# RWKV-7's chunk outputs: 128-row and 64-row products issued as two runs instead of alternating

## The chip, the cores and the metric

The kernel runs on one NeuronCore of one Trainium2 chip. The metric is the device time of one execution in microseconds (us); lower is better. A time is the median of several executions. The profile is of one further execution.

## The reference, cut to what matters

The reference is a two-layer encoder on 256 tokens of 1024 features. Each layer is a SwiGLU feed-forward, then three token mixers side by side (RWKV-7, Hyena, Mamba-2 SSD) that share one input projection and one output projection, then a second SwiGLU. The change touches the RWKV-7 mixer alone, whose recurrence is, per head of 64 channels and in both directions of time:

```python
def rwkv7_step(S, inp):
    r_t, w_t, k_t, v_t, a_t, b_t = inp
    sa = jnp.einsum('dbhij,dbhj->dbhi', S, a_t)
    S = S * w_t[..., None, :] + sa[..., None] * b_t[..., None, :] + v_t[..., None] * k_t[..., None, :]
    return S, jnp.einsum('dbhij,dbhj->dbhi', S, r_t)
```

The scan runs over 256 tokens, for 8 heads and 2 directions, in each of the 2 layers. The output of a token is the state `S` applied to the receptance `r_t`.

## The kernel before, in words

Everything is kept feature-major: features on the 128 partitions, tokens along the free axis. The large projections and the feed-forwards are dense products, 128 x 128 weights against 256 tokens, each done in three passes over split operands (`mm3`, tiles named `psd` in the profile). Their weights are loaded by SyncE's queue (`raw`), rounded to the first part on ScalarE (`whi`, L278) and the second part is made on VectorE or GpSimd (`wlo`, L308).

RWKV-7 is done in chunks of 64 tokens, four chunks per sequence, and in two waves (w = 0, 1) of two head pairs each. `rw_invert` inverts the triangular blocks of a wave on GpSimd (L886, L888). `rw_chain` then goes over the four chunks, i = 0 to 3. It holds eight instances at a time: u = 0 to 3 (direction and pair) times e = 0, 1 (the head of the pair, on partitions 0 to 63 or 64 to 127; `HALF[e]`). One step i is, on TensorE,

- `pr`: eight products of 128 rows (scores against removal values and values), copied by VectorE to `rw_rhs` (L968);
- `pu`: eight products of 64 rows with the inverses `zt`, copied into `se` and `so` by VectorE (L973) and ScalarE (L974);
- `pn` (not in the last step): eight products of 128 rows, from which VectorE makes the next state `new`; VectorE and ScalarE copy it into the operands of the next step (L991, L992);
- `py`: the outputs of the chunk. For each of the eight instances one product of 128 rows (`ss` against the scores `gg`, written G below) and, from the second chunk on (`st` is not None), one product of 64 rows (the state `st` against the receptances `ar`, written S below) into the same 64 x 64 sum. ScalarE copies `py` to `yd` (L1002).

All of them are float32 and have 64 output columns; head e = 0 writes partitions 0 to 63 of the bank and e = 1 the other half. A float32 product shows as two MATMUL records and two LDWEIGHTS records in the profile, so one step's `py` is 16 products and 32 records where there is a state and 8 products and 16 records where there is none. In records the operands read as `128*64 128x64` for `pr`, `pn` and G, and as `64*64 64x64` for `pu` and S; `pu` carries the name `rw_rhs`.

The order on each engine is planned at build time: the framework takes the program order as priority, simulates the engines (`schedule_with_timeline_sim=True`, L1456) and lets independent work run between the steps of the chain. TensorE's time between them is filled with dense products of the projections and with SSD's products (`pss`). The chains run at about 423 to 487 us (layer 0, wave 0), 512 to 590 us (layer 0, wave 1), 1261 to 1327 us and 1350 to 1426 us (layer 1).

Of the kernel before, what the change touches and what calls it, by code (L numbers as in the profile page):

```python
"""Two hybrid encoder layers (SwiGLU, RWKV-7 / Hyena / SSD mixers, SwiGLU) on one core.

Everything is kept feature-major: [feature in a tile of 128, tile, token].  Products run as three
float32r passes over exactly split operands (hi * hi + hi * lo + lo * hi)."""
# [20 lines left out]
# columns of SBUF: the mixers' arena, its part that is given up after RWKV-7, a block within it, the  # L25
# arena of the set up
ARENA, AHEAD, BLK, START = 63 * 256, 65 * 256, 7 * 1024, 16 * 1024
# what outlives the part that is given up; the grid of places within an arena
KEEP, GRID = ("blk", "y0", "y1", "mg"), 256
# products of the next sublayer that start before the LayerNorm's statistics are known  # L30
NE = 4
# units of the mixers' output projection that are loaded and split ahead
NPRE = 1
# LayerNorm, by tile: h on ScalarE, the mean taken off on GpSimd; the tile whose split comes before
# the early products are made up
HACT, SUBP, EA = (0, 1, 1, 1, 0, 1, 1, 1), (0, 0, 1, 1, 1, 1, 1, 1), 3
# adaLN chunks computed alongside each sublayer; buffers for those in the mixers; rows multiplied on GpSimd
# there; tiles of ones in the start up that have buffers of their own; the output tile of a SwiGLU at which
# all have to be done
NSIDE, NRING, SPOOL, NRAW, SIDEM = (4, 2, 4, 4, 1, 1), 3, (0, 0, 0, 0, 1, 0, 1, 0), 4, 3  # L40
# order of the projections: gates, dt, SSD tiles; gates, Hyena
SEQ = ("g" * 10 + "d" + "s" * 12, "g" * 14 + "h" * 8)
# one in so many splits of weights goes to GpSimd (0: none), by part of the mixers
# [12 lines left out]
def layout(inp):  # L56
    """Inputs as DRAM arrays, moved into the order in which the kernel reads them."""
# [47 lines left out]
def constants():  # L105
    """Tables that follow from the shapes alone."""
# [36 lines left out]
class Arena:  # L143
    """A region of SBUF in which arrays are placed; the framework orders what overlaps."""

    def __init__(self, *aps):
        self.aps, self.clock = [], len(aps)
        self.holes, self.live = [], {}
        for ap in aps:
            o = self.aps[-1][0] + self.aps[-1][1] + 1 if self.aps else 0  # L150
            self.aps.append((o, ap.shape[1], ap))
            self.holes.append((o, ap.shape[1]))
        # when each column was given back last
        self.freed = np.zeros(o + ap.shape[1], int)
        for i, (o, n, _) in enumerate(self.aps):
            self.freed[o:o + n] = i

    def drop(self):
        """The last part is given up; it has to be empty."""
        o, n, _ = self.aps.pop()  # L160
        assert (o, n) in self.holes, (o, self.live)
        self.holes.remove((o, n))

    def take(self, name, shape):
# [4 lines left out]
        # the columns that have been free for longest  # L169
# [35 lines left out]
def spread(items, counts):  # L205
    """The items in order, as lists of so many each."""
    items = iter(items)
    return [[next(items) for _ in range(n)] for n in counts]


class Builder:
# [42 lines left out]
    def dbank(self):  # L254
        """A bank for one dense product."""
        return self.bank("d", 4)[:, 0:256]

# [33 lines left out]
    def mm(self, out, lhsT, rhs, start, stop):  # L291
        return self.nc.tensor.matmul(out, lhsT, rhs, start=start, stop=stop)  # L292
# [4 lines left out]
    def after(self, later, *earlier):  # L297
        """Issue order on one engine."""
        for e in earlier:
            self.tc.add_manual_dep(later.ins, e.ins.name, ORDER, reason="issue order")  # L300
# [9 lines left out]
    def unit(self, dram, width=1024, ahead=None):  # L310
        """One unit of weights, loaded and split."""
# [30 lines left out]
    def dense_pair(self, outs, ws, x):  # L342
        """Two products that follow x tile by tile as it comes."""
        for k in range(NT):
            for out, w in zip(outs, ws):
                self.mm3(out, w, k * 128, x[k], k == 0, k == NT - 1)

# [39 lines left out]
    def cond_row(self):  # L387
        """silu(c) on every partition."""
# [65 lines left out]
    # ---- residual + LayerNorm; tiles of the sublayer's output come through ln_put().  All are  # L454
    # centred by the mean of the first one's features: the mean of all differs from it by at most
    # sqrt(7) standard deviations, so that the sums of squares keep their accuracy ----
# [18 lines left out]
    def u_put(self, m):  # L475
        """The tile as it enters the products that start before the statistics are known."""
        if self.nxt in self.mods:
            assert (*self.nxt, 0) in self.done and (*self.nxt, 1) in self.done
            a, hi = self.mods[self.nxt][:, 24 + m:25 + m], self.uh[:, m, 0:256]
            self.act(hi, self.r[:, m, :], AF.Identity, scale=a)  # L480
            self.stt(self.ul[:, m, 0:256], self.r[:, m, :], a, hi.bitcast(F32), MUL, SUB)

    def early(self, units, ahead):
        """The next sublayer's first products, of a * r instead of a * (r - mean) * rstd + b; two
        more columns take -a and b through the weights, from which early_end() makes them up."""
# [9 lines left out]
    def early_end(self, mu, rs, prev):  # L495
        """(product - mu * first column) * rstd; the second column is left as a bias."""
# [9 lines left out]
    def ln_put(self, m, psum):  # L506
# [5 lines left out]
        if m == 0:  # L512
# [4 lines left out]
            # the tiles that are still to come are centred through xa  # L517
# [151 lines left out]
    def shift(self, l, dst, i, spread=False):  # L669
        """The token shift; spread: on ScalarE and GpSimd."""  # L670
# [14 lines left out]
    def conv(self, l, dst, i, wn, bn, taps, n, j):  # L685
        """A centred depthwise convolution of projection tile i; n tiles of channels, this one is j."""
# [45 lines left out]
    def rw_keys(self, s):  # L732
        """Decays, gates and keys of both directions, scaled within chunks of 64."""
# [6 lines left out]
        # normalised keys  # L740
# [25 lines left out]
        # cumulative decays in chunks of 64, taken from their middle  # L766
# [14 lines left out]
        # scaled receptances and removal keys; keys and removal values  # L781
# [8 lines left out]
        # what the bonus sums  # L790
# [7 lines left out]
    def rw_scores(self, s):  # L798
# [13 lines left out]
        for d in (0, 1):  # L812
# [17 lines left out]
            # scores  # L830
# [18 lines left out]
            # keys token-major  # L849
# [11 lines left out]
            # removal keys over the first block of the scores  # L861
# [9 lines left out]
    def rw_invert(self, s):  # L871
        """Unit triangular inverses of 32 x 32 blocks, one a lane (direction, half, instance, head)."""
# [18 lines left out]
        # zout[0]: the inverses, zout[1]: transposed  # L891
# [7 lines left out]
    def rw_chain(self, s):  # L899
# [4 lines left out]
        # values token-major  # L904
# [13 lines left out]
        # the inverses, transposed, on the diagonals of 64 x 64 blocks, and those that join them  # L918
# [16 lines left out]
        # joined into 64 x 64 blocks  # L935
# [21 lines left out]
        # the chain over four chunks  # L957
# [4 lines left out]
        for i in range(4):  # L962
# [12 lines left out]
            if i < 3:  # L975
# [5 lines left out]
                # the factor between chunk c and the next one in this direction  # L981
# [10 lines left out]
                nc.scalar.copy(out=so[64:128, :, i + 1, :], in_=new[64:128])  # L992
            py = bank("m", 2).rearrange("p (u q) -> p u q", q=64)
            for u in range(4):
                c = 3 - i if u > 1 else i
                for e in (0, 1):
                    self.mm(py[HALF[e], u, :], ss[e][:, u, i, :], gg[e][u // 2][:, u % 2, i, 64:128], True, st is None)
                    if st is not None:
                        self.mm(py[HALF[e], u, :], st[HALF[e], u, :], ar[HALF[e], u // 2, u % 2, c], False, True)
# [8 lines left out]
    def rw_out(self, s):  # L1008
        """Group norm over heads, bonus, gate."""
# [41 lines left out]
    def ssd_proj(self, l):  # L1051
# [9 lines left out]
        # dt = softplus, and the running sums of its decays within chunks of 128  # L1061
# [29 lines left out]
    def ssd_tiles(self, l):  # L1091
        """Twice the SiLU, as (1 + tanh(x / 2)) x."""
# [16 lines left out]
    def ssd(self, l):  # L1109
        nc, A, F, bank, scol = self.nc, self.A, self.F, self.bank, self.scol  # L1110
        # x * dt token-major, for each direction
        self.yc = []
        for g in (0, 1):
# [12 lines left out]
            # C B^T, masked where it is on the diagonal  # L1126
# [9 lines left out]
            for e in range(4):  # L1136
# [6 lines left out]
                for d in (0, 1):  # L1143
# [3 lines left out]
                    # from the other chunk: d = 0 from 0 into 1, d = 1 from 1 into 0  # L1147
# [32 lines left out]
    def hy_sin(self, x):  # L1180
        """sin of x in place, brought into [-pi, pi] first."""
# [20 lines left out]
    def hy_filter(self):  # L1202
        """Spectra of the filters of both layers, kept in DRAM, and their norms."""
# [101 lines left out]
    def gates(self, l):  # L1305
        """tanh(x / 2) of the gates' projections, kept in DRAM: twice the gate is one more."""
# [154 lines left out]
```

## Time and profile before

| | |
|---|---|
| time, three runs | 1717.62, 1721.4, 1725.15 us; median 1721.4 us |
| span of the profiled execution | 1726.7 us, 35017 instructions |
| TensorE (PE) busy | 1599.4 us, 93% of the span, 13142 matmul records |
| PE's weight loads (PEld) busy | 1494.3 us, 87% |
| VectorE (DVE) busy | 1319.2 us, 76% |
| ScalarE (ACT) busy | 946.2 us, 55% |
| GpSimd (POOL) busy | 599.8 us, 35% |
| chain that ended last, by engine | PE 68%, DVE 17%, DMA 5%, ACT 4%, POOL 3% |
| mean granted TensorE clock | 0.956 of full speed |

The page gives the profiled execution's span, from its first to its last instruction, and no separate time around it; the span lies 5.3 us above the median of the three runs. A busy TensorE is not a TensorE at its peak: the end of each matmul is modelled, so the pace of a run of matmuls is read from the starts, or from the chain of waits, which cuts time where the next instruction starts. The granted clock has two levels in these rows, 1.2 GHz (0.50) and 2.4 GHz (1.00); a value between them is a mix within the stretch.

### The profile page before, as it was taken

The numbers are of one execution on the slowest core, as the hardware profiler recorded it, in microseconds if no ns is written. First come the engines' busy times: TensorE is split into PE (matmuls) and PEld (weight loads), VectorE is DVE, ScalarE is ACT, GpSimd is POOL, SyncE is SP. The second block draws the span as 40 slices with busy tenths as digits, with TensorE's granted clock in tenths as the row PEclk, the third lists the DMA queues.
The fourth block names the chain that finished last, engine by engine and source line by source line (L and its number), as shares of the span: only waits on it lengthen the run. The fifth ranks groups of instructions, "written<-read, shape, count | busy, mean of one in ns | idle before, by whom it ended". The sixth has DMA issues, their size and how long they took to land.

```text
span 1726.7 us, 35017 instructions
## 1 busy us (share of the span) xinstructions
PE 1599.4 (93%) x13142; PEld 1494.3 (87%) x13142; DVE 1319.2 (76%) x2392; ACT 946.2 (55%) x1838; POOL 599.8 (35%) x598
## 2 busy tenths in 40 slices
PE   5999997989999988999999999988989998889996
PEld 2999987878888877999999999877878887889996
DVE  6888878598668587988889887768965836887665
ACT  2655567546465535655575556745635634465554
POOL 0000048396725556100020002757674334640001
PEclk9999998889998999999999999989999978999998
DMA  9888753536467454888769886344555635557663
GB/s 364 298 286 301 253 189 120 153 106 171 129 190 253 159 178 159 310 306 299 234 238 349 289 282 208 129 124 127 128 162 165 211 131 164 162 185 243 219 179 92
DMA packets 157896, 355.94 MB, mean 206 GB/s; under 512 B 55901, under 2 KB 75806, under 8 KB 157471
## 3 DMA queue, kind: packets, MB, share of 16 engines
q1 hardware_dynamic: 157726, 353.71, 62.1%
q8 instruction: 103, 1.69, 0.4%
q14 instruction: 67, 0.54, 0.1%
HBM read 332.11 MB, written 18.91 MB: 203 GB/s over the span
## 4 chain that ended last, share of the span: by engine, by line
PE 68%; DVE 17%; DMA 5%; ACT 4%; POOL 3%; issue 3%; SPq 0%; ACTq 0%; DVEq 0%; POOLq 0%
PE psd L292 55%; PE psm L292 9%; PE pss L292 4%; DVE arena L281 4%; DVE arena L289 3%; DVE wlo L308 2%; ACT whi L278 1%; DMA raw<-in_win 1%; DVE r L281 1%; POOL arena L888 1%; POOL arena L886 1%; DVE hlo L308 1%; ACT arena L278 1%; DVE arena L770 1%; POOL wlo L308 1%
## 5 line engine op out<-in xcount | busy, mean ns | idle before, releaser
L278 ACT ACTIVATE whi<-raw 128x512 fp32r<-128x512 f32 (+1 forms) x846 | 519.2, 621 | 426.9 <-PE psd L292 334.0
L292 PE MATMUL psd<-hhi,wlo 128*128 128x256 f32 (+1 forms) x2288 | 667.5, 292 | 20.4 <-POOL wlo L308 12.4
L292 PE MATMUL psd<-hhi,whi 128*128 128x256 f32 x2288 | 665.2, 291 | 9.2 <-ACT whi L278 6.0
L292 PE MATMUL psd<-hlo,whi 128*128 128x256 f32 x2288 | 662.2, 290 | 0.0
L308 DVE TENSOR_TENSOR wlo<-raw,whi 128x512 fp32r<-128x512 f32 x632 | 450.8, 720 | 157.6 <-ACT whi L278 138.7
L308 POOL TENSOR_TENSOR wlo<-raw,whi 128x512 fp32r<-128x512 f32 x214 | 300.7, 1416 | 697.4 <-ACT whi L278 650.2
L292 PEld LDWEIGHTS psd<-hhi,wlo 128*128 128x128 f32 (+1 forms) x2288 | 449.5, 197 | 31.6 <-POOL wlo L308 14.2
L292 PEld LDWEIGHTS psd<-hhi,whi 128*128 128x128 f32 x2288 | 449.5, 197 | 17.8 <-issue 7.0
L292 PEld LDWEIGHTS psd<-hlo,whi 128*128 128x128 f32 x2288 | 449.9, 197 | 4.8 <-issue 2.7
L292 PE MATMUL psd<-alo,whi 128*128 128x256 f32 x704 | 199.1, 283 | 0.0
L292 PE MATMUL psd<-ahi,wlo 128*128 128x256 f32 x704 | 197.4, 280 | 0.0
L292 PE MATMUL psd<-ahi,whi 128*128 128x256 f32 x704 | 197.4, 280 | 0.0
L551 POOL TENSOR_TENSOR r<-r,lmu 128x256 f32<-128x256 f32 x36 | 31.3, 902 | 352.5 <-ACT lmu L278 352.5
L289 DVE SCALAR_TENSOR_TENSOR ada_raw<-ada_raw,cond 128x1024 f32<-128x1024 f32 x104 | 128.7, 1238 | 30.1 <-DMA ada_raw<-in_ada 29.9
L292 PEld LDWEIGHTS psd<-ahi,wlo 128*128 128x128 f32 x704 | 133.9, 190 | 0.3
L292 PEld LDWEIGHTS psd<-alo,whi 128*128 128x128 f32 x704 | 132.7, 189 | 0.3
L292 PEld LDWEIGHTS psd<-ahi,whi 128*128 128x128 f32 x704 | 132.2, 188 | 0.1
L292 PE MATMUL psm<-arena 64*128 64x128 f32 (+6 forms) x824 | 102.6, 270 | 17.3 <-DVE arena L289 7.1
L278 ACT ACTIVATE arena<-arena 128x512 f32<-128x512 f32 (+4 forms) x108 | 65.9, 619 | 88.6 <-DVE arena L281 26.3
L292 PEld LDWEIGHTS psm<-arena 64*128 64x128 f32 (+4 forms) x824 | 72.0, 156 | 37.0 <-DVE arena L289 8.5
L292 PE MATMUL pss<-arena 128*64 128x128 f32 (+3 forms) x326 | 81.8, 403 | 23.3 <-ACT arena L278 8.6
L292 PEld LDWEIGHTS pss<-arena 128*64 128x64 f32 (+2 forms) x326 | 50.2, 178 | 43.8 <-issue 16.9
(217 smaller groups left out, 2470.4 us busy)
## 6 DMA issues: line engine op xcount, KB each, us to landing
raw<-in_wi SPq DMA_DIRECT2D x176, 512.0 KB, 4.5
raw<-in_win SPq DMA_DIRECT2D x126, 512.0 KB, 3.8
ada_raw<-in_ada SPq DMA_DIRECT2D x104, 512.0 KB, 5.2
raw<-in_wo SPq DMA_DIRECT2D x64, 512.0 KB, 3.8
arena<-in_ada SPq DMA_DIRECT2D x32, 512.0 KB, 5.4
raw<-in_wo SPq DMA_DIRECT2D x32, 384.0 KB, 3.3
raw<-in_pab SPq DMA_DIRECT2D x24, 512.0 KB, 3.6
raw<-in_wout SPq DMA_DIRECT2D x16, 512.0 KB, 4.3
```

What stands on the lines that cost most here:

```text
L278: return self.nc.scalar.activation(out=out, in_=in_, func=func, **k)
L281: return self.nc.vector.tensor_tensor(out=out, in0=a, in1=b, op=op)
L289: return self.nc.vector.scalar_tensor_tensor(out=out, in0=a, scalar=s, in1=b, op0=op0, op1=op1, **k)
L292: return self.nc.tensor.matmul(out, lhsT, rhs, start=start, stop=stop)
L308: return self.act(hi, src, AF.Copy), (eng or self.nc.vector).tensor_tensor(out=lo, in0=src, in1=hi.bitcast(F32), op=SUB)
L551: x = sub_(out=r[:, m, :], in0=r[:, m, :], in1=mu[:], op=SUB)
L770: nc.vector.tensor_tensor_scan(cum[:, d, p], self.scm[:], sig[:, d, p], 0.0, op0=MUL, op1=ADD)
L886: g.tensor_tensor(out=tv, in0=zw[:, j + 1:32, j:j + 1].to_broadcast([64, n, j]), in1=zw[:, j:j + 1, 0:j].to_broadcast([64, n, j]), op=MUL)
L888: g.tensor_tensor(out=zw[:, j + 1:32, 0:j], in0=zw[:, j + 1:32, 0:j], in1=tv, op=ADD)
```

## The change

Only the order of the sixteen products of `py` and their start flags change. Before, each S product followed its G product. After, the eight G products are issued first and the eight S products after them. A product's `start` flag was true for each G; now it is true for u = 0 alone (one for each head, that is, for each half of the bank's partitions), and the other products rely on that one start. The helper `mm` passes further arguments on, and a check on accumulation groups is switched off for these products. The rest of the diff replaces comments by blank lines.

```diff
-    def mm(self, out, lhsT, rhs, start, stop):
-        return self.nc.tensor.matmul(out, lhsT, rhs, start=start, stop=stop)
+    def mm(self, out, lhsT, rhs, start, stop, **k):
+        return self.nc.tensor.matmul(out, lhsT, rhs, start=start, stop=stop, **k)
...
             py = bank("m", 2).rearrange("p (u q) -> p u q", q=64)
             for u in range(4):
-                c = 3 - i if u > 1 else i
                 for e in (0, 1):
-                    self.mm(py[HALF[e], u, :], ss[e][:, u, i, :], gg[e][u // 2][:, u % 2, i, 64:128], True, st is None)
-                    if st is not None:
-                        self.mm(py[HALF[e], u, :], st[HALF[e], u, :], ar[HALF[e], u // 2, u % 2, c], False, True)
+                    self.mm(py[HALF[e], u, :], ss[e][:, u, i, :], gg[e][u // 2][:, u % 2, i, 64:128], u == 0, st is None,
+                            skip_group_check=True)
+            if st is not None:
+                for u in range(4):
+                    c = 3 - i if u > 1 else i
+                    for e in (0, 1):
+                        self.mm(py[HALF[e], u, :], st[HALF[e], u, :], ar[HALF[e], u // 2, u % 2, c], False, True,
+                                skip_group_check=True)
             for d in (0, 1):
                 c = 3 - i if d else i
                 nc.scalar.copy(out=yd[:, d, :, 64 * c:64 * c + 64], in_=py[:, 2 * d:2 * d + 2, :])
```

## Rows read from the trace of the kernel before

**Rows 1.** The ending chain between 434 and 512 us, share by line.
```profile
by line: PE psd L292 48.8%; PE psm L292 28.7%; PE pss L292 19.9%; DVE arena L281 1.7%; DVE arena L289 0.6%; PE pss L1118 0.6%; issue 0.1%
```

**Rows 2.** The ending chain in time, 400 to 1440 us: start, us, what ran.
```profile
465.38 4.46 PE psm L292 x46
...
544.28 7.10 PE psm L292 x46
...
585.45 4.11 PE psm L292 x32
...
1382.78 6.98 PE psm L292 x46
```

**Rows 3.** Timeline of PE inside one `py`: start, us, line, operation, operands, count.
```profile
465.31 0.69 PE L292 MATMUL psm<-arena,arena 128*64 128x64 f32 x16
465.93 0.32 PE L292 MATMUL psm<-arena 64*64 64x64 f32 x2
466.18 0.33 PE L292 MATMUL psm<-arena,arena 128*64 128x64 f32 x2
466.44 0.33 PE L292 MATMUL psm<-arena 64*64 64x64 f32 x2
```

**Rows 4.** Timeline of PE: runs of one shape, each with the row after it.
```profile
432.72 1.15 PE L292 MATMUL psm<-arena,arena 128*64 128x64 f32 x30
433.80 0.39 PE L292 MATMUL psd<-hlo,whi 128*128 128x256 f32 x1
...
456.27 0.69 PE L292 MATMUL psm<-arena,arena 128*64 128x64 f32 x16
456.89 0.39 PE L292 MATMUL psd<-hlo,whi 128*128 128x256 f32 x1
...
477.36 0.68 PE L292 MATMUL psm<-rw_rhs,arena 64*64 64x64 f32 x16
477.97 0.39 PE L292 MATMUL psd<-hhi,wlo 128*128 128x256 f32 x1
```

**Rows 5.** Timeline of PE before and in the block at 544 us (a bracket: idle before).
```profile
542.40 0.33 PE L292 MATMUL psm<-arena,arena 128*64 128x64 f32 x2 [2.71 <-DVE arena L973]
...
544.22 1.01 PE L292 MATMUL psm<-arena,arena 128*64 128x64 f32 x13
...
545.27 0.88 PE L292 MATMUL psm<-arena,arena 64*64 64x64 f32 x4
```

**Rows 6.** PE by stretch: us, PE busy (records), granted clock, DMA share, GB/s.
```profile
451.49:454.25 2.76, 2.76 (x14) 0.50 0.66 190
551.40:559.50 8.10, 8.10 (x48) 0.66 0.48 160
573.80:578.30 4.50, 4.50 (x26) 0.62 0.39 123
1290.80:1293.50 2.70, 2.70 (x13) 0.50 0.15 61
1389.75:1394.60 4.85, 4.85 (x28) 0.65 0.10 16
1407.96:1412.30 4.34, 4.34 (x21) 0.50 0.00 0
1425.19:1431.50 6.31, 6.31 (x33) 0.57 0.08 27
...
589.60:593.30 3.70, 3.70 (x32) 1.00 0.14 42
```

**Rows 7.** Stages: us, busy of PE, PEld, DVE, ACT, POOL, then clock, DMA share, GB/s.
```profile
423.00:512.00 89.00, 86.43 (x841) 75.72 (x841) 62.39 (x133) 49.82 (x94) 52.99 (x63) 0.98 0.52 163
...
1380.00:1425.00 45.00, 43.70 (x352) 37.89 (x352) 17.65 (x47) 15.09 (x30) 15.38 (x12) 0.80 0.39 133
```

**Rows 8.** Who waited for whom, ScalarE: total us, times, longest.
```profile
ACT arena L1002 <- PE psm L292: 43.6, 12, 6.9
```

**Rows 9.** Timeline of DVE and PE around the next step after one block.
```profile
574.02 0.29 DVE L991 COPY arena<-arena 64x256 f32<-64x256 f32 x1
...
578.27 0.27 PE L292 MATMUL psm<-arena 128*64 128x64 f32 x1
```

## The prediction

> **What bounds the kernel now.** I read the ending chain first, over the whole span and then around RWKV-7's four chains. Between 434 and 512 us TensorE's lines hold 98% of it [rows 1], and in order of time the blocks named "psm x46" and "psm x32" are among its longest single pieces [rows 2]. They are `pn` with `py`, and `py` of the last step alone. So a microsecond taken out of such a block is a microsecond off the chain, as long as nobody else becomes late. The stages tell who could: in 423 to 512 us TensorE is busy for 86.43 of 89 us, VectorE for 62.39, GpSimd for 52.99, ScalarE for 49.82; in 1380 to 1425 us, a second wave, it is 43.70 of 45 against 17.65, 15.38 and 15.09 [rows 7].
>
> The timeline inside one block shows why it is long. After sixteen records of 128 rows, pairs of 64-row and 128-row records alternate, and the starts lie 0.25, 0.26 us apart: one product takes 0.26 us [rows 3]. The same two shapes in runs of their own go much faster: sixteen records (eight products) of 128 rows hold TensorE from 456.27 to 456.89, 0.62 us, and sixteen of 64 rows (`pu`) from 477.36 to 477.97, 0.61 us [rows 4], under 0.08 us a product. What costs is the change of shape between them.
>
> **The change part by part.** *The order of sixteen products.* Nothing is added or removed: the same 32 matmul and 32 weight-load records per block, the same copies, no DMA, and no new wait, since `st` and `ar` are ready before the G products are. Only blocks with a state have S products: three steps times two waves times two layers, twelve blocks. The first step's eight products stay a run as they were.
>
> Eight of the twelve follow `pn`, whose products have the shape of G. In the chain such a block is 46 records (fourteen of 128 rows that remain of the run, then the alternating 32) and takes 4.46 us at full clock [rows 2]. After the change it is 30 records of 128 rows and 16 of 64. The trace has a run of 30: 432.72 to 433.80, 1.08 us [rows 4]. With 0.61 for the run of 64 rows that makes 1.69, a saving of 4.46 - 1.69 = 2.77 us.
>
> Four blocks belong to the last step, with no `pn`: 32 records, 4.11 us [rows 2]. They become 0.62 + 0.61 = 1.23, a saving of 2.88.
>
> Two of the eight ran at the lower clock from start to end, 7.10 and 6.98 us [rows 2]. There a run of sixteen 128-row records took 544.22 to 545.27, 1.05 us, against 0.62 at full clock, a factor of 1.7 [rows 4, 5]; 1.69 becomes 2.87 and they save 4.23 and 4.11.
>
> Sum: 6 x 2.77 + 4.23 + 4.11 + 4 x 2.88 = 36.5 us of TensorE time. (Some of the full-clock blocks are a little longer than the ones I use, because the clock falls inside them; I leave that to the next term.) Bounds: a run of S products that accumulate into sums begun by others isn't in the trace. Its lower bound is the 0.61 of `pu`, its upper one the 8 x 0.26 = 2.1 us that eight products take in the alternation. I take 0.61, because `pu` has the same shape, the same halves and one bank. With 2.1 for S alone the sum falls by 12 x 1.5 = 18, to 18.5 us.
>
> The Trainium skill speaks against the 0.61: "TensorEngine Tiling (Array Packing)", Gotcha 1 (PSUM Pressure), says that products on different row groups can't use the same PSUM bank at the same time. The two heads of S lie on different row halves and write one bank; by this rule they would run one after the other, say 1.22 us a run, and the gain would shrink by 12 x 0.61 = 7 us. The run of `pu`, with exactly this layout, took 0.61, no longer than 0.62 for products over all rows [rows 4], so here the trace does not show it.
>
> *The clock after the blocks.* Behind seven of the twelve blocks the granted clock stood wholly or partly at 1.2 GHz for 2.70 to 8.10 us while TensorE worked without a gap [rows 6]. Work at clock share c loses (1 - c) of its time: 1.38 + 2.75 + 1.71 + 1.35 + 1.70 + 2.17 + 2.71 = 13.8 us. Before the falls TensorE was in the alternation, where it finished few products. But the last block of layer 0, wave 1, was followed by 1.00 [rows 6], so the alternation alone does not decide. In two of the seven the clock was already low at the block's start, after 2.71 us in which TensorE waited for VectorE [rows 5]; that wait isn't touched, and I give back half of their 4.45. Of the other five (9.3) I take three quarters, 7. Together 9 us; bounds 0 and 13.8.
>
> *What is late next.* ScalarE stood 43.6 us in twelve waits for `py` before L1002 [rows 8], with weight roundings queued behind; these come earlier with the block, so the splits follow TensorE. VectorE's copy of the state (L991) is not tied to the end of `py`: in one place it ends at 574.31 and the next `pr` starts at 578.27, 3.96 us later [rows 9]. There the block's 2.77 and up to 1.71 of clock come off ahead of it, so TensorE may wait some 0.5 us. Weight loads move earlier at a DMA share of 0.52 [rows 7], which leaves room. GpSimd has the inversion of wave 1 besides its splits, but 36 us of slack in 89 [rows 7]. I charge 3 us in all for such small waits; bounds 0 and 17 (the first rival).
>
> Result: 36.5 + 9 - 3 = 42.5 us. The profiled span of 1726.7 becomes 1684.2; that span lies 5.3 above the median of 1721.4, so I predict 1679 us.
>
> **The rivals.** *The other engines take half of it.* In the first wave of layer 0 VectorE, GpSimd and ScalarE each work 50 to 62 of 89 us [rows 7]; if the weight splits there can't follow a faster TensorE, it reaches the same wait later in the stage and wave 0's saving, 2 x (2.77 + 2.77 + 2.88) = 17 us, is lost, along with the clock's part. What is left is wave 1's: 9.88 + 9.76 = 19.6, a time of 1702 us. For it: VectorE is at 70% there. Against: the chain of the first of these stretches is TensorE's [rows 1], and ScalarE idles in front of each `py` [rows 8].
>
> *It doesn't do what it says.* If 0.26 us were the price of a short product that adds to an open sum and not of the change of shape, nothing goes: 1721 us. Against: in the alternation the G products, which begin their sums, are as slow as the S ones [rows 3], and the same G shape in a run is not [rows 4].
>
> *Slower, through the plan.* The order on all engines is planned from a simulation of the whole program. New ready times in each chunk may place chain steps and VectorE's Hyena and modulation work differently, so that TensorE arrives early at a step of the chain, stands still and goes on at the lower clock. The trace has such a place at 542.40: 2.71 us idle, then a low clock [rows 5, 6]. Its price is 2.71 for the wait, about half of the 7.10 us block and 2.75 for the stretch behind it, 9 us. To end slower by the 8.6 us that count as slower, five such stalls more than today are needed ((36.5 + 8.6) / 9): 1730 us. Against: the products and their number stay, so the plan has little reason to change far from the block.
>
> **How the numbers follow.** My forecast has 0.69, with its own range of 1665 to 1694; the half-hidden case 0.19, 1702; no effect 0.06; the plan 0.06. The fastest end is 36.5 + 13.8 with no new wait, 1671, less the 9 us of a stall that happens to go away, 1662. The slow end covers the half-hidden case with a few microseconds to spare, 1706. About 0.5%, 8.6 us, is what a measurement of this kernel can tell from no change: faster 0.88, same 0.06, slower 0.06.
>
> **What would show it.** In the profile after, a `py` block should read as one row of 30 (or 16) records of 128 rows and one of 16 records of 64 rows, 1.7 or 1.2 us together at full clock, and no alternating pairs. ScalarE's wait of L1002 for TensorE should fall from 43.6 us to about 15. The clock behind the blocks should be 1.00 in most places. TensorE's busy time should fall by some 45 us while its count of matmuls stays. The prediction is wrong if the blocks are short but the chains' ends (487 and 590 us) come less than 8 and 15 us earlier, or if TensorE's idle time grows by more than a few microseconds.

## The result, and the profile after

The changed kernel takes 1694.07 us (1692.41 to 1696.84, 4 runs) against 1721.46 us before: a ratio of 0.9847 with a 95% interval of 0.9812 to 0.9882, 27.4 us faster. In a second comparison, with 6 runs of it and 17 of the kernel before, it was 1696.1 against 1723.8 us, 0.9858 (0.9828 to 0.9888). The forecast was 1679 us. The time lies inside the whole range of 1662 to 1706 us, but at the very end of the main case's own range (1665 to 1694) and nearer to the first rival's 1702 than to 1679; the gain is a little under two thirds of the one forecast. Times here and below are medians of fast executions (of the old order with the new flags one execution in ten took 3725 us and is left out).

The page of the changed kernel, its span and the first line of part 1:

```profile
span 1691.8 us, 35016 instructions
PE 1554.2 (92%) x13142; PEld 1461.7 (86%) x13142; DVE 1319.6 (78%) x2392; ACT 945.7 (56%) x1838; POOL 597.7 (35%) x598
```

The count of matmuls is unchanged. TensorE's busy time fell by 1599.4 - 1554.2 = 45.2 us, the span by 1726.7 - 1691.8 = 34.9. The difference, 10.3 us, is new idle time of TensorE.

The ending chain of the changed kernel in layer 1's wave 1 (start, us, what); these lines answer to [rows 2]:

```profile
1365.68 2.18 PE psm L292 x46
...
1379.68 1.69 PE psm L292 x46
...
1392.28 1.22 PE psm L292 x30
```

A full-clock block of 46 records takes 1.69 us, one of the last step 1.22, to the hundredth what the runs of [rows 4] had given. The first of the three started at the lower clock and was done in 2.18 instead of 2.87.

TensorE's timeline at the end of the second of these blocks, where [rows 3] had alternating pairs, with the row after it:

```profile
1380.69 0.68 PE L292 MATMUL psm<-arena,arena 64*64 64x64 f32 x16
1381.30 0.39 PE L292 MATMUL psd<-hhi,wlo 128*128 128x256 f32 x1
```

The sixteen S records are one run of 0.61 us (1380.69 to 1381.30).

ScalarE's wait for `py`, and the clock behind blocks (us, PE busy, clock, DMA share, GB/s), which answer to [rows 8] and [rows 6]; the line number has moved by 6:

```profile
ACT arena L1008 <- PE psm L292: 8.7, 6, 2.4
```

```profile
454.00:458.70 4.70, 3.44 (x32) 1.00 0.26 68
545.40:553.00 7.60, 7.60 (x63) 0.86 0.85 286
...
1381.40:1383.90 2.50, 2.50 (x22) 1.00 0.58 162
```

ScalarE waits 8.7 us instead of 43.6. Behind eleven of the twelve blocks the clock is 1.00; the second line is the one exception, behind a block that already began low. In the first line TensorE is busy for 3.44 of 4.70 us: one of the new waits.

Where the waits are shows in the stage of wave 0, from the first `rhs` copy of wave 0 to the first of wave 1. First the kernel before, then the changed one (us, PE busy, clock, DMA share, GB/s):

```profile
423.10:514.10 91.00, 88.53 (x926) 0.98 0.52 163
1261.30:1351.50 90.20, 87.15 (x896) 0.96 0.48 149
```

```profile
431.00:519.20 88.20, 81.85 (x933) 0.98 0.56 171
1247.40:1334.30 86.90, 79.26 (x895) 0.96 0.53 158
```

TensorE's work in the stage shrank by 6.7 and 7.9 us, the stage only by 2.8 and 3.3. The chain itself kept its saving. These are ScalarE's copies of the last `py` in layer 0's wave 0, before and after:

```profile
486.51 0.43 ACT L1002 COPY arena<-psm 128x128 f32<-128x128 f32 x2 [2.84 <-PE psm L292]
```

```profile
485.42 0.43 ACT L1008 COPY arena<-psm 128x128 f32<-128x128 f32 x2 [0.70 <-PE psm L292]
```

From its first copy to this one the chain took 63.4 us before and takes 54.4 now (in layer 1 64.9 and 56.1). The stretch from there to wave 1's first copy grew instead, from 27.6 to 33.8 us and from 25.3 to 30.8: the stage holds nearly the same matmuls as before (926 and 933 records), and what no longer fits between the chain's steps runs behind them.

Wave 1's stages (first copy to 8 us after its last S) went the other way round:

```profile
514.10:597.00 82.90, 78.24 (x674) 0.90 0.65 225
1351.50:1434.00 82.50, 78.98 (x661) 0.86 0.50 172
```

```profile
519.20:585.30 66.10, 60.62 (x647) 0.97 0.77 266
1334.30:1401.30 67.00, 64.43 (x677) 0.97 0.62 215
```

They are 16.8 and 15.5 us shorter, against a direct saving of 9.9 and 9.8. Most of the rest is the clock, which had cost 0.10 x 82.9 + 0.14 x 82.5 = 19.8 us before and costs 4.0 now. (The sum does not close exactly: the direct saving already holds 2.8 us of clock, from the two blocks that ran at the lower one, and the stages hold 27 records fewer and 16 more than before.)

In wave 0's stage of layer 0, what the changed kernel's TensorE waited for (total us, times, longest):

```profile
PE pss L292 <- DVE arena L281: 2.8, 4, 1.3
PE psm L292 <- DVE arena L973: 1.4, 2, 0.7
PE psm L292 <- issue: 1.1, 1, 1.1
PE psm L292 <- DVE rw_rhs L968: 0.7, 1, 0.7
```

The largest is SSD's: its products (`pss`) wait until VectorE has multiplied the decay factors by C B^T (L281). In layer 1 this wait was there before the change too (2.2 us, now 2.7). There the longest new one is 2.65 us, for which the view names no releaser ("issue"):

```profile
1326.66 0.68 DVE L281 TENSOR_TENSOR arena<-arena,psm 128x512 f32<-128x512 f32 x1
1327.44 0.74 PE L292 MATMUL psm<-arena 32*32 32x32 f32 x64 [2.65 <-issue]
```

These are the products of 32 rows with which wave 1's chain prepares its inverses. They begin 0.10 us behind the end (1327.34) of the multiplication by the gate in wave 0's output stage, which reads a `psm` bank on VectorE. The 1.1 us of "issue" in layer 0 lie at the same place (508.28, behind 508.18), and so do the waits in the second profile of the changed kernel and in that of wave 0 alone, below. That the products wait for this bank is the likely reading; no run takes that wait away alone.

Not all that happened lies in the chains. The changed kernel's first copy in layer 0 comes 7.9 us later (431.0 against 423.1), before there is any `py`, and behind a stretch with a lower clock, first before, then after (us, PE busy, clock, DMA share, GB/s):

```profile
380.00:400.00 20.00, 18.88 (x141) 0.93 0.55 162
```

```profile
380.00:400.00 20.00, 18.15 (x106) 0.68 0.47 136
```

The second profile of the changed kernel shows the same (first copy at 430.6, clock 0.67). In the twelve profiles of all other orders, the kernel before included, that copy comes at 423.1 to 427.5 and the clock is 0.85 to 1.00. TensorE's products up to there come in the same order before and after, so it is probably the plan of the other engines that differs; no run isolates it. From the first copy to the end the kernel before takes 1726.7 - 423.1 = 1303.6 us and the changed one 1691.8 - 431.0 = 1260.8, 42.8 less.

### The profile page after: what moved, and what is told of

Read it like the earlier page. It is cut to its first block, busy times and chain, and to the rows that moved or that the text cites. A ratio compares the mean times of both kernels' runs of the same rounds, so it can differ in the third digit from the quotient of the medians.

```text
span 1691.8 us, 35016 instructions
## 1 busy us (share of the span) xinstructions
PE 1554.2 (92%) x13142; PEld 1461.7 (86%) x13142; DVE 1319.6 (78%) x2392; ACT 945.7 (56%) x1838; POOL 597.7 (35%) x598
## 3 DMA queue, kind: packets, MB, share of 16 engines
q8 instruction: 103, 1.69, 0.4%
## 5 line engine op out<-in xcount | busy, mean ns | idle before, releaser
L308 DVE TENSOR_TENSOR wlo<-raw,whi 128x512 fp32r<-128x512 f32 x632 | 440.2, 703 | 150.1 <-ACT whi L278 132.4
L292 PE MATMUL psm<-arena 64*128 64x128 f32 (+6 forms) x824 | 88.3, 266 | 22.5 <-DVE arena L289 7.1
L292 PE MATMUL pss<-arena 128*64 128x128 f32 (+3 forms) x326 | 78.2, 388 | 27.5 <-ACT arena L278 8.5
L292 PEld LDWEIGHTS psm<-arena 64*128 64x128 f32 (+4 forms) x824 | 65.7, 157 | 38.0 <-issue 13.2
```

Source lines behind the costliest of these rows:

```text
L308: return self.act(hi, src, AF.Copy), (eng or self.nc.vector).tensor_tensor(out=lo, in0=src, in1=hi.bitcast(F32), op=SUB)
```

## The experiments

The theory: the price was the change of shape; the blocks are short now; what is missing of the gain was lost in wave 0's stage, where SSD's masked products hang on VectorE and cannot come earlier. The rivals: the price sat in the start flags or in the S products, or both waves gave equally little.

**The change once more**, beside the next three.

> The changed kernel once more, as the measure for the three beside it. 1690 to 1698 us, 24 to 31 us below the kernel before, if the first comparison stands.

1696.1 us (1693.53 to 1702.86), 0.9858 (0.9828 to 0.9888). As expected.

**One wave at a time.** The new order under a condition, the old order (with the new flags) otherwise:

```diff
+            if w == 0:        # e3_wave1: w == 1
+                ... the two runs
+            else:
+                ... G and S alternating
```

> Two runs in wave 0 alone, alternating order in wave 1. Theory: TensorE's saving in wave 0 (2 x 8.4 us direct) is mostly lost again before wave 1 starts, because SSD's masked products there hang on VectorE and on the loads of the decay rows; 3 to 8 us remain: 1713 to 1718 us. Rival: the two waves are worth the same, half of the whole gain each: 1706 to 1709 us.

> Two runs in wave 1 alone, alternating order in wave 0. Theory: nearly all of the gain sits here, 19.6 us direct and some of the clock behind the blocks: 1695 to 1701 us. Rival: half of the whole gain: 1706 to 1709 us.

Wave 0 alone: 1715.15 us, 0.995 (0.9927 to 0.9973), 8.6 us faster. Wave 1 alone: 1699.7 us, 0.9868 (0.9841 to 0.9894), 24.1 us faster. Equal halves are out; wave 0 gave 0.6 us more than the upper end of what I had expected. The sum, 32.7, is above the 27.7 of both together, within what the intervals allow; on top of wave 1's change, wave 0's was worth 3.5 us. Wave 0's stages in the profiles, first with the two runs in wave 0 alone, then in wave 1 alone:

```profile
426.90:515.80 88.90, 83.28 (x945) 0.98 0.56 169
1251.80:1339.40 87.60, 79.44 (x896) 0.96 0.51 154
```

```profile
427.50:516.10 88.60, 87.01 (x915) 0.98 0.55 160
1251.10:1340.30 89.20, 85.42 (x895) 0.98 0.50 153
```

TensorE is idle for 5.6 and 8.2 us where wave 0 has the short blocks and for 1.6 and 3.8 where it has the long ones, in stages of nearly the same length. The waits come with wave 0's change, in the very stage.

**The decay rows in halves.** The changed kernel, with the rows that SSD spreads over the partitions loaded one head at a time into two half-size buffers:

```diff
-                if e % 2 == 0:
-                    vb = A("svb", 2, 2, 256)
-                    for d in (0, 1):
-                        self.dma(vb[:, d], self.vrow[d, h:h + 2, :].unsqueeze(0).to_broadcast([128, 2, 256]))
+                vb = A(f"svb{e % 2}", 2, 256)
+                for d in (0, 1):
+                    self.dma(vb[:, d], self.vrow[d, h:h + 1, :].to_broadcast([128, 256]))
...
```

> The changed kernel with SSD's decay rows loaded one head at a time into two buffers of half the size, instead of two heads at a time into one buffer, so that a load need not wait until both heads before it are done. Theory (these loads eat wave 0's saving): 3 to 8 us below the changed kernel, 1686 to 1691 us, and VectorE's wait for the rows, 9.6 us in layer 0's wave 0, down to under 4. Rival (another wait takes their place, or twice as many loads cost as much): within 2 us of the changed kernel.

1697.2 us, 0.986 (0.9834 to 0.9887): no different from the change alone. But VectorE's wait did not fall as I had expected. Its row in wave 0 of layer 0, first of the changed kernel, then of this one:

```profile
DVE arena L286 <- DMA arena<-vrow: 9.6, 5, 2.9
```

```profile
DVE arena L286 <- DMA arena<-vrow: 8.4, 4, 3.6
```

In layer 1 it rose, from 3.9 to 7.4 us. So the experiment did not take away what it was to take away, and it says nothing about whether that wait matters. (The wait before the 32-row products is gone in this profile, and TensorE still idles for 6.6 and 6.5 us in wave 0's stages: others took its place.) The same edit on the kernel before was to be its control:

> The kernel before with SSD's decay rows loaded one head at a time into two half-size buffers. Theory (before the change TensorE was late in that stage, not the rows): within 3 us of the kernel before. Rival (the rows already held up the kernel before): 4 us or more below it.

1725.7 us, 1.0015 (0.999 to 1.004): no change there either.

**The old order with the new flags.**

```diff
             for u in range(4):
                 c = 3 - i if u > 1 else i
                 for e in (0, 1):
                     ... G, start = (u == 0)
                     if st is not None:
                         ... S
```

> The old alternating order with the new start flags (one start per head instead of eight). Theory (the price is the change of shape, the flags are free): the time of the kernel before within 4 us, blocks of 46 records at 4.46 us at full clock. Rival (the many starts cost): 8 us or more below the kernel before.

1722.3 us (nine executions) against 1722.1, 1.0009 (0.997 to 1.0049). Its chain has the old block, and the flags are worth nothing that can be seen:

```profile
1290.76 4.46 PE psm L292 x46
```

**Shorter runs.** Two products of each kind in turn, and four:

```diff
             for u in range(4):          # e7_fours: for two u at a time
                 for e in (0, 1):
                     ... G
                 for e in (0, 1) if st is not None else ():
                     ... S
```

> G, G, S, S: the two heads of a u together, 8 runs of two products a block instead of 16 of one. Theory (each change of shape costs the same, (4.11 - 1.23) / 14 = 0.206 us): a block of 32 records takes 1.23 + 6 x 0.206 = 2.47 us, one of 46 records 2.92, and 16 of the 27 us are gained: 1703 to 1709 us. Rival (S products are slow wherever they are short of a full run): 3.3 us or more a block of 32, under 10 us gained.

> Four G, four S, four G, four S: 4 runs a block. Theory: a block of 32 records takes 1.23 + 2 x 0.206 = 1.64 us, one of 46 records 2.10, and 22 to 26 of the 27 us are gained: 1695 to 1700 us. Rival (only an unbroken run is fast): 2.4 us or more a block of 32.

Pairs: 1697.7 us, 0.9849 (0.9807 to 0.9891). Fours: 1697.1 us, 0.9833 (0.9799 to 0.9866). The timeline of a block of pairs, then of fours:

```profile
1287.60 0.80 PE L292 MATMUL psm<-arena,arena 128*64 128x64 f32 x18
1288.32 0.33 PE L292 MATMUL psm<-arena 64*64 64x64 f32 x4
1288.59 0.34 PE L292 MATMUL psm<-arena,arena 128*64 128x64 f32 x4
...
1290.16 1.13 PE L292 MATMUL pss<-arena,cst 128*128 128x256 f32 x4
```

```profile
1284.36 0.91 PE L292 MATMUL psm<-arena,arena 128*64 128x64 f32 x22
1285.20 0.45 PE L292 MATMUL psm<-arena 64*64 64x64 f32 x8
1285.58 0.45 PE L292 MATMUL psm<-arena,arena 128*64 128x64 f32 x8
...
1286.34 1.13 PE L292 MATMUL pss<-arena,cst 128*128 128x256 f32 x4
```

The run is what costs, but not in proportion to the changes of shape. A run of one product takes 0.26 us [rows 3], of two 0.27, of four 0.38, of eight 0.61: from two on, about 0.15 us for the run and 0.06 for each product. A product alone costs as much as two: in a run the records of the two heads start 7 ns apart, so the second head's product comes at almost no cost. That S adds to a sum just written is not the price, since G runs, which begin sums, last as long: 0.26 us from 1288.59 to the next start at 1288.85, against 0.27 for the S run before. The block of 46 records takes 2.56 us in pairs (2.92 expected) and 1.98 in fours (2.10), against 4.46 and 1.69. Pairs have 1.9 of the 2.77 us a block and all of the measured gain: my expectation for them, 1703 to 1709, missed. Between 2.6 and 1.7 us a block, TensorE's time in the blocks no longer shows in the total, as far as four executions each can tell (the intervals reach some 7 us to either side).

**SSD's work on VectorE made lighter**, in both orders. The multiplication by C B^T is left out:

```diff
-                self.tt(fw, fw, cb.rearrange("p a s t -> p (a s t)"), MUL)
```

> The changed kernel without SSD's multiplication of the decay factors by C B^T (1.36 us of VectorE per head, 16 heads in all; the output is another). For the pair with e10. Theory (in wave 0's stage VectorE's work for SSD is what TensorE waits for once the blocks are short): the gain of the change grows when VectorE has less to do there, from 27 us to 32 to 38 us between e10 and e9, and TensorE's idle time in each wave 0 falls from 6.5 and 8.9 us to under 5. Rival (the waits sit at the chain's own copies, whatever SSD does): the difference stays at 23 to 30 us and the idle time does not fall.

> The kernel before without the same multiplication. Theory: TensorE was late in that stage before the change, so VectorE's relief is worth little there: 0 to 6 us below the kernel before. Rival: 8 us or more below it.

With the change 1690.6 us, 0.9815 (0.9774 to 0.9856); without it 1731.2 us, 1.0034 (1.0006 to 1.0062). The change is worth 40.6 us here instead of 27. (The 1.36 us of the expectation is the first head's in each layer; the mean of the sixteen before is 1.03.) Wave 0's stages (us, then busy of PE, PEld, DVE, ACT, POOL), first with the change, then without:

```profile
426.70:518.00 91.30, 84.92 (x956) 75.51 (x956) 62.34 (x139) 54.83 (x103) 53.73 (x62) 0.98 0.63 196
1245.10:1342.60 97.50, 89.48 (x978) 80.56 (x978) 70.07 (x144) 57.52 (x108) 55.51 (x62) 0.96 0.61 193
```

```profile
425.90:524.90 99.00, 95.77 (x968) 84.35 (x969) 65.30 (x144) 58.16 (x109) 53.06 (x63) 0.97 0.58 180
1264.10:1372.60 108.50, 99.90 (x974) 87.99 (x974) 70.87 (x144) 58.34 (x108) 55.79 (x62) 0.94 0.55 176
```

The stages shrink by 7.7 and 11.0 us, where they had shrunk by 2.8 and 3.3, about wave 0's direct saving of 8.4. That is for the theory. Against it: TensorE is still idle for 6.4 and 8.0 us in them, where I had expected under 5 and the rival no fall, and the kernel without the change grew slower by VectorE's relief, where I had expected a gain of up to 6 us. The plan answered to the lighter work by putting more of it into these stages (974 matmul records where there were 896), so that the pair does not isolate VectorE. I count it as support, not as proof.

**Two attempts at a better version.** Pairs in wave 0 and two runs in wave 1; and the S products right behind `pu`, ahead of `pn`:

```diff
+            py = bank("m", 2).rearrange("p (u q) -> p u q", q=64)
+            if st is not None:
+                ... S, start = (u == 0)
             nc.vector.tensor_copy(out=se[0:64, :, i, :], in_=pu[0:64, 0:4, :])
...
-            py = bank("m", 2).rearrange("p (u q) -> p u q", q=64)
             ... G, start = (u == 0 and st is None)
```

> Pairs (G, G, S, S) in wave 0, two runs in wave 1: an attempt at a version better than both, since in single profiles the pairs had the shorter wave 0 (85 and 82 against 88 and 87 us) and the two runs the shorter wave 1 of layer 0 (58 against 70 us). If these differences belong to the order of the products: 1680 to 1688 us. If they come from how the whole program was planned around it: 1692 to 1702 us, as the others.

> The eight S products issued right behind pu, whose shape they share, ahead of pn; G then follows pn's run. Two changes of shape fewer a block (some 0.15 us each, 12 blocks, 3.6 us) and a shorter wait of ScalarE for py. Theory (TensorE's time in the blocks is no longer what decides): within 4 us of the changed kernel. Rival (each change of shape still counts in full): 4 us or more below the changed kernel.

The mixture: 1697.6 us, 0.9847 (0.9802 to 0.9891), nothing beyond the change; the stage lengths that had suggested it belong to the plan around the block, not to its order (wave 1 of layer 0 took 70 us here too, with two runs). The early S products: 1686.9 us (1678.68 to 1692.93), 0.9787 (0.9743 to 0.983). It is 35 us faster than the kernel before. Against the change it was not timed side by side; from the two ratios to the kernel before, 0.9787 / 0.9858 = 0.993, with half-widths of 0.004 and 0.003 that add in squares to 0.005, the difference is just clear, 7.5 us by the medians and 12 by the ratios. My expectation, within 4 us, missed. Its S products share `pu`'s shape and form one run with them:

```profile
1280.05 0.68 PE L292 MATMUL psm<-rw_rhs,arena 64*64 64x64 f32 x16
1280.56 0.63 PE L292 MATMUL psm<-arena 64*64 64x64 f32 x16
1281.16 0.32 PE L292 MATMUL pss<-arena 128*64 128x128 f32 x1
```

`pu` and S take 1.11 us and a run of 30 G records 1.08 [rows 4], 2.19 together, against 0.61 + 1.69 = 2.30 before it. Twelve times 0.11 is 1.3 us, not the 7.5 to 12 by which it is ahead, so the rival's price is not borne out either. In the profiles the lead does not lie in the chains. Its stages, wave 0 and wave 1 of layer 0, then of layer 1 (wave 1's again to 8 us behind the last block):

```profile
425.30:506.70 81.40, 76.66 (x903) 1.00 0.54 163
506.70:584.00 77.30, 69.04 (x695) 0.96 0.77 257
1246.30:1328.40 82.10, 77.71 (x906) 0.98 0.55 166
1328.40:1397.00 68.60, 63.15 (x662) 0.98 0.63 211
```

Wave 0's are shorter than the changed kernel's (88.2 and 86.9), wave 1's longer by about as much (66.1 and 67.0 there). From the first copy to the end it takes 1687.5 - 425.3 = 1262.2 us, the changed kernel 1260.8 and 1265.2 in its two profiles. What it is ahead by in the profiles, 4.3 and 8.3 us, is there for the most part when the first chain starts: 425.3 against 431.0 and 430.6 us, with a clock of 0.93 from 380 to 400 us against 0.68 and 0.67. So the early S products may have gained next to nothing themselves. The executions without a profile can't be split in this way.

## Why the prediction was right, and where its size was off

*The price of the alternation*: shown. The old order with the new flags has the old time and the old block; runs of two, four and eight shorten the block step by step. *Its size*: 1.69 and 1.22 us a block were met exactly. The S products of both heads, on different rows and into one bank, ran together as `pu` had: their records start 7 ns apart, and the run takes 0.61 us, not the 1.22 that the prediction had weighed against it.

*The clock behind the blocks*: right in direction. In the pair of profiles wave 1's stages lost 19.8 us to it before and 4.0 after. The other profiles bear it out: in the five where wave 1 alternates, its stages lost 10 to 20 us, in the nine where it has runs of two, four or eight, 2 to 7. But the size was read from one execution. Two further profiles of the alternating order show less loss than the first, that with the new flags, then that with the halved rows:

```profile
516.00:598.00 82.00, 77.58 (x672) 0.90 0.66 224
1354.10:1432.00 77.90, 73.30 (x672) 0.96 0.57 187
```

```profile
521.30:603.70 82.40, 75.22 (x670) 0.96 0.68 226
1356.80:1436.80 80.00, 74.24 (x651) 0.91 0.51 172
```

That is 11.3 and 10.5 us, not 19.8. The execution that I worked from lay above the median: after the change a run's time is 1.8 us above its span (1693.58 for 1691.8), so 1726.7 stands for about 1728.5 us, 7 above the median. Its mean clock of 0.956 says why. Of the 53 executions of the kernel before that were timed beside the experiments, the six with a clock under 0.958 took 1726 to 1733 us, the fifteen with 0.966 or more 1711 to 1724. I moved the level by 5.3 us for that and left the gain as it was; part of what I counted as gain was that execution's own.

*Small waits, 3 us*: this term failed in size. TensorE's idle time grew by 10.3 us in the pair of profiles, most of it in wave 0's stages (3.9 and 4.6). The first rival had named the place, and half of its loss came: wave 0 alone is worth 8.6 us of the 17 us saved there. It had not named the waits: in layer 0's stage TensorE waits 0.3 us for weight splits (1.2 before); the longest new ones are SSD's and, as far as shown, that for a bank.

*The slower plan* came in part, and in a place that the prediction had not thought of: the 7.9 us ahead of the first chain. Elsewhere, too, plans differ: wave 1 of layer 0, from its first copy to its last S, took 58 us after the change and 70 with pairs, with wave 0 the shorter there.

Together: 42.5, less 7.3 for the waits, less 7 for that execution, is 28.2 us; 27.4 were measured. That this closes is partly luck. The term for the clock held too little for wave 1 in this pair of profiles (15.8 us) and nothing for the loss ahead of the first chain, and the two errors offset each other.

By two of its own signs the prediction was wrong. Wave 0's and wave 1's chains in layer 0 were to end at least 8 and 15 us earlier and ended 1.1 and 12.0 us earlier (485.4 and 577.6 us); TensorE's idle time was to grow by no more than a few microseconds. The blocks were right; the start of the first chain and the waits behind it were not, and the time is inside the range because the range reached to the first rival.

What stays open: which of wave 0's waits decides (the lighter SSD supports VectorE's part, the halved rows missed their target, the wait for a bank was not tested), and why the clock fell ahead of the first chain in both profiles of the changed kernel.

## What to carry to other kernels

Look in the timeline for small matmuls of two shapes that alternate: here a lone product cost 0.26 us and one in a run 0.06 to 0.08, so sort them by shape, and put a run beside another one of its shape. Shortening TensorE's work pays in full only where the other engines have slack: wave 1's stage kept everything, wave 0's gave half of it or more back to waits that the trace of before hardly showed, since TensorE had covered them. Read the clock's losses from more than one execution before they go into a sum. And when two planned kernels are compared, look first at where they part: here several microseconds of difference stood ahead of the first place that the change touches.

## What was not expected of the hardware

A run of two products, one for each half of the bank, took 0.27 us, as long as one product alone (0.26). So half of the loss was gone with pairs already. And in wave 1's stages before the change six blocks of 4 to 7 us went with a granted clock of 0.90 and 0.86; with blocks of 1.2 to 2.4 us it was 0.97, though TensorE had more idle time in the whole. The alternation alone does not do it: in this pair of profiles wave 0's six blocks alternated before as well, and the clock over its stages was 0.98 and 0.96, the same as after.
